# Moving the loads of the units' weights from SyncE's queue to ScalarE's, 0.3 slots later, in a hybrid attention block

## The chip, the cores and the metric

The kernel runs on one core of a Trainium2 chip. The metric is the device time of one execution in microseconds, as the median of several runs. The names of the engines are those of the profile: PE (TensorE), PEld (its weight loads), DVE (VectorE), ACT (ScalarE), POOL (GpSimd) and SP (SyncE, which computes nothing here and only issues DMAs).

## The reference

One layer works on x of 2048 tokens by 1024 channels in float32. What it computes, cut to what matters:

```python
h = rms_norm(x, norm_gain)
proj = h @ w_in                      # q, k, v of two mixers, gate paths, merge gates
qa, ka, va, qb, kb, vb, ga, gb, mg = split(proj)
ya = banded_attention(norm(qa) * scale, norm(ka), va, 128, 1, bias, sink) * silu(ga)
for g, (window, dilation) in enumerate(((128, 1), (512, 4), (2048, 16))):
    outs[g], lses[g] = dilated_group(norm(qb[g]) * scale, norm(kb[g]), vb[g], window, dilation, bias)
yb = sum(softmax(lses) * outs) * silu(gb)
merged = sigmoid(mg_a + b) * (ya @ w_branch_a) + sigmoid(mg_b + b) * (yb @ w_branch_b)
out = x + merged @ w_out
```

## The kernel before

Every product that needs float32 accuracy is made of float16 halves: an operand is split into a high and a low part, and three matmuls (high x high, low x high, high x low) replace one. The normed input lies in SBUF as XH and XL.

**Units and slots.** The main loop has 14 units (`UNITS`): two of mixer A and twelve of mixer B, each with 384 columns of the input projection, that is, the q, k and v of a few heads. A unit has 8 slots; in each slot a `Pair` projects two blocks of 128 tokens (2 x 24 matmuls of 384 columns, L709), and the attention of earlier blocks is worked off in between. Some slots also carry a fill: a product of the gate paths (L333).

**From projection to attention.** ACT takes the projection out of PSUM (`evac_qk` L726, `v_hi` L735) and DVE ends that with `v_lo` (L741). The bank is then free for PE; there are two such banks (`pj`). q and k are normed, split (ACT L777, DVE L781), swapped (POOL L786) and turned by a DMA transpose into the ring `kq` (`turn`, L794, issued by SP). The scores (L879) read `kq`. Then come bias and maximum (DVE L894), exponentials (ACT L902), their two halves (ACT L907, DVE L911) and another DMA transpose into `pt` (L917, SP). The values' product (L928) reads that, and ACT evacuates it (L951, L956, L960). For two of mixer B's three groups the result `z` is stored to DRAM (`z_store`, L967) by a DMA that ACT issues; all other DMAs are issued by SP.

**The units' weights.** While unit u runs, the weights of unit u+1 are made ready. `w_load` (L182 to L188) loads them in four quarters of 384 KB into the one buffer `wraw`; POOL multiplies each quarter with the norm's gain (`w_gain`, L193), ACT sums squares (L235), and ACT and DVE split it (L252, L258). The buffer `wraw` also serves other loads within a unit (gate weights, L347; pieces of other weights, L1137), so a load first waits for its last reader. Index u+1 = 14 loads the first of the merge gates' weights (`w_mrg`, quarters of 256 KB), index 15 the second; index 0 is loaded before the main loop.

**What sets the order.** Nothing is scheduled automatically. Every step is put with `at(time, f)` into a heap, the time in slots, and the program is recorded in the order of these times; each engine works its instructions off in that order. `W_STEP` and `B_GAP` place the weights' steps: quarter i of unit u+1 is loaded at slot 8u + W_STEP[0] + 0.25 i, its gain is due from 8u + 1.558 on, 0.445 slots apart. So a DMA that waits holds up everything that its issuing engine has queued behind it. All DMAs share eight semaphores in turn, so an issue also waits until the DMA eight places earlier in the program has landed.

Of the kernel before, what the change touches and what calls it, by code (L numbers as in the profile page):

```python
# [61 lines left out]
NU = len(UNITS)  # L62
# [13 lines left out]
Y_DMA = (-0.097, 0.45, 0.55, 1.05, 1.13, 1.2, 1.25)  # L76
Y_MAX_DMA = (0.026, 1.4, 1.45)
GATE = (-0.123, -0.064, 0.329)
W_STEP = (0.1, 0.465, 1.9, 0.445, 4.197, 0.146, 0.342)
W_MAX = (3.762, 3.892)  # L80
G_PREP = (5.907, 6.882, 7.102, 7.671, 7.712, 7.812, 7.942)
N_PREP = (6.3, 7.15, 7.753)
# [41 lines left out]
def block_kernel(tc, x, w_units, w_gate, w_mrg, w_brn, w_out, w_bra, gain, qkg, sink, bias_a, bias_b, b_merge, out):  # L124
    nc = tc.nc
# [53 lines left out]
    def raw_tile():  # L179
        return wp.tile([128, NCH, 384], F32, name="wraw", bufs=1)  # L180

    def w_load(u, parts=(0, 1, 2, 3)):  # L182
        if u not in wtiles:
            wtiles[u] = [raw_tile()]
        raw = wtiles[u][0]
        src, n = (w_units[u], 384) if u < NU else (w_mrg[u - NU], 256)
        for i in parts:
            nc.sync.dma_start(out=raw[:, 2 * i:2 * i + 2, :n], in_=src[:, 2 * i:2 * i + 2, :])  # L188

    def gains(raw, c0, n):  # L190

# [243 lines left out]
    def chain(steps):  # L435

        steps = sorted(steps, key=lambda e: e[0])
        done = [0]

        def go(k):  # L440
            if done[0] < k or steps[k][1](*steps[k][2:]) is False:
                at(now[0] + .04, go, k)
            else:
                done[0] = k + 1

        for k, e in enumerate(steps):
            at(e[0], go, k)
# [140 lines left out]
    for i in range(4):  # L588
        at(X_W["ld"][i], w_load, 0, (i,))
# [8 lines left out]
    for pos, c, q, halves in X_MM:  # L598
# [5 lines left out]
        n = 256 * len(halves)  # L604
# [558 lines left out]
    for u in range(NU + 1):  # L1163
        t = 8 * u
        steps = [(t + W_STEP[0] + B_GAP[0] * i, w_load, u + 1, (i,)) for i in range(4)]
        for i in range(4):
            steps += [(t + W_STEP[2] - W_STEP[6] + W_STEP[3] * i, w_gain, u + 1, i),
                      (t + W_STEP[2] + W_STEP[3] * i, w_square, u + 1, i),
                      (t + W_STEP[4] + W_STEP[3] * i, w_hi, u + 1, i),
                      (t + W_STEP[4] + W_STEP[5] + W_STEP[3] * i, w_lo, u + 1, i)]  # L1170
        chain(steps + [(t + d, f, u + 1) for d, f in zip(W_MAX, (w_sum, w_pow))])
# [12 lines left out]
    for k in range(8):  # L1184
        u = 3 + k
# [13 lines left out]
    while t < NPAIR or heap or any(k >= t for k in fill):  # L1199
        u, j = divmod(t, 8)  # L1200
# [211 lines left out]
    def prep(t, u):  # L1412
        sq = [(t + T_W[0], w_load, u), (t + T_W[5], w_sum, u), (t + T_W[6], w_pow, u)]
        for i in range(4):
            sq += [(t + T_W[1] + T_W[2] * i, w_gain, u, i), (t + T_W[3] + T_W[4] * i, w_square, u, i),
                   (t + T_W[7] + T_W[8] * i, w_hi, u, i), (t + T_W[7] + T_W[8] * i + T_W[9], w_lo, u, i)]
        chain(sq)
# [436 lines left out]
```

## Time and profile before

| what | value |
|---|---|
| median of 3 runs (lowest, highest) | 1915.26 us (1915.14, 1917.81) |
| profiled execution, its own time | 1916.12 us |
| its span, first to last instruction | 1914.3 us |
| DMA packets, mean rate over the span | 316.56 MB, 165 GB/s |
| time of SP's queue as a share of 16 DMA engines | 69.2% |
| time of ACT's queue as a share of 16 DMA engines | 2.0% |
| DMAs that ACT issues | 128, all of L967, 66 KB each |
| loads of L188 for the units' weights | 56, 384 KB each; 24 more of 256 KB for `w_mrg` |

How to read it: "q1" in the page is SP's queue and "q10" ACT's. The time from a DMA's issue to its landing is another thing than the duration of the issuing instruction; the profile gives both, the second on the issuing engine's row. A DMA share over 1 is possible in a window, because a packet counts for the time between its start and its end, and packets of one engine overlap.

### The profile page before, as it was taken

The page shows a single profiled execution, that of the slowest core. Times are in us where ns is not written, and L with a number is a line of the kernel's source. Part 1 is how long each engine was busy: PE and PEld are TensorE (multiplying, and loading weights), DVE is VectorE, ACT ScalarE, POOL GpSimd, SP SyncE. Part 2 cuts the span into 40 slices and gives each one's busy share as a digit, 9 for nine tenths or more (in the row PEclk, how much of TensorE's full clock was granted, in tenths as well). Part 3 has the DMA queues.
Part 4 walks back from the last instruction along what each step waited for, and adds up shares of the span by engine and source line. Part 5 has one row for each costly group of instructions (what it writes and reads, how often), then busy time and mean ns, then how long its engine had stood idle before and what let it go on. Part 6 is the DMA issues. An engine that isn't in the chain of part 4 may idle for free.

```text
span 1914.3 us, 39281 instructions
## 1 busy us (share of the span) xinstructions
PE 1899.4 (99%) x13578; PEld 1190.4 (62%) x13578; DVE 1360.3 (71%) x3522; ACT 1120.4 (59%) x2496; POOL 843.7 (44%) x1848
## 2 busy tenths in 40 slices
PE   8999999999999999999999999999999999999999
PEld 6566666677666688566787667876544444444444
DVE  8578886887767877577776877768686667767312
ACT  8468776787656776566766767666544545323100
POOL 4333454344545655446555565555412211223543
DMA  8459986897968697578768788766822346778763
GB/s 285 128 107 181 194 166 152 149 199 151 189 104 197 131 186 139 116 158 175 168 123 155 160 174 150 130 118 132 186 75 99 105 154 220 223 245 261 265 226 138
DMA packets 624585, 316.56 MB, mean 165 GB/s; under 512 B 492928, under 2 KB 562176, under 8 KB 623104
## 3 DMA queue, kind: packets, MB, share of 16 engines
q1 hardware_dynamic: 605952, 305.39, 69.2%
q10 hardware_dynamic: 18432, 8.66, 2.0%
q8 instruction: 106, 1.74, 0.4%
q14 instruction: 95, 0.78, 0.2%
HBM read 129.91 MB, written 65.27 MB: 102 GB/s over the span
## 4 chain that ended last, share of the span: by engine, by line
PE 86%; DVE 5%; DMA 3%; POOL 2%; issue 2%; ACT 2%; SPq 0%; DVEq 0%; POOLq 0%; ACTq 0%
PE pj L709 37%; PE pj L333 15%; PE fps L333 11%; PE fps L1721 6%; PE s L879 5%; PE pv L928 4%; PE fps L1516 3%; DMA kq<-spl 2%; PE pj L1721 2%; PE pj L609 2%; PE pj L1516 1%; DVE p L911 1%; DVE pr L894 1%; DVE qss L753 1%; DVE rw L765 0%
## 5 line engine op out<-in xcount | busy, mean ns | idle before, releaser
L709 PE MATMUL pj<-wh,XL 128*128 128x384 f16 x1792 | 586.1, 327 | 0.0
L709 PE MATMUL pj<-wh,XH 128*128 128x384 f16 x1792 | 584.5, 326 | 1.4 <-DVE vt L741 1.4
L709 PE MATMUL pj<-wl,XH 128*128 128x384 f16 x1792 | 584.7, 326 | 0.0
L709 PEld LDWEIGHTS <-XH 128*128 128x128 f16 x3584 | 410.5, 116 | 151.9 <-issue 1.7
L894 DVE CUSTOM_DVE_ANT_0 pr<-s,b,ubuf 128x256 f32<-128x256 f32 (+3 forms) x512 | 219.1, 465 | 81.1 <-PE s L879 79.3
L709 PEld LDWEIGHTS <-XL 128*128 128x128 f16 x1792 | 207.7, 116 | 70.3 <-issue 1.2
L911 DVE SCALAR_TENSOR_TENSOR p<-pr,p 128x512 f16<-128x512 f32 (+2 forms) x256 | 189.5, 740 | 20.2 <-ACT p L907 20.0
L786 POOL COPY spl<-spl 128x256 f16<-128x256 f16 (+1 forms) x224 | 88.1, 423 | 185.7 <-DVE spl L781 184.3
L726 ACT ACTIVATE rw<-pj 128x256 f32<-128x256 f32 (+1 forms) x224 | 86.8, 388 | 138.3 <-PE pj L709 124.2
L907 ACT ACTIVATE p<-pr 128x512 f16<-128x512 f32 (+2 forms) x256 | 159.2, 622 | 6.2
L333 PEld LDWEIGHTS <-wh 128*128 128x128 f16 x960 | 93.7, 98 | 110.5
L879 PE MATMUL s<-kq 128*128 128x256 f16 (+3 forms) x1168 | 147.8, 254 | 2.9 <-DMA kq<-spl 2.9
L928 PEld LDWEIGHTS <-pt 128*128 128x128 f16 x3024 | 125.4, 97 | 34.8
L286 POOL TENSOR_TENSOR rs_t<-rs_y 128x8 f32<-128x8 f32 (+1 forms) x112 | 40.2, 359 | 238.4 <-DVE rs_y L278 189.6
L771 POOL TENSOR_TENSOR rw<-rw,g 128x256 f32<-128x256 f32 (+1 forms) x112 | 90.8, 811 | 109.9 <-DVE rw L765 76.1
L193 POOL TENSOR_TENSOR wraw<-wraw,gn 128x768 f32<-128x768 f32 (+1 forms) x80 | 112.5, 1411 | 55.5 <-DMA wraw<-in_w_mrg_dram 43.6
L928 PE MATMUL pv<-vt,pt 128*128 128x65 f16 (+1 forms) x3024 | 132.7, 192 | 0.0
L879 PEld LDWEIGHTS <-kq 128*128 128x128 f16 x1184 | 101.5, 98 | 45.5 <-DMA kq<-spl 4.4
L765 DVE TENSOR_TENSOR rw<-rw,qr 128x512 f32<-128x512 f32 (+1 forms) x112 | 103.6, 925 | 30.8 <-POOL qr L295 29.9
L741 DVE SCALAR_TENSOR_TENSOR vt<-pj,vt 128x128 f16<-128x128 f32 (+1 forms) x224 | 62.1, 277 | 88.3 <-ACT vt L735 87.4
L333 PE MATMUL pj<-XH,gh 128*128 128x512 f16 x320 | 121.3, 379 | 0.0
L333 PE MATMUL pj<-XH,gl 128*128 128x512 f16 x320 | 121.2, 379 | 0.0
(281 smaller groups left out, 3799.0 us busy)
## 6 DMA issues: line engine op xcount, KB each, us to landing
wraw<-in_w_units_dram SPq DMA_DIRECT2D x56, 384.0 KB, 4.8
mtd<-mm SPq DMA_DIRECT2D x56, 256.0 KB, 3.7
M<-mtd SPq DMA_DIRECT2D x8, 1792.0 KB, 9.5
mgd<-fg SPq DMA_DIRECT2D x39, 256.0 KB, 2.1
zd<-z ACTq DMA_DIRECT2D x128, 66.0 KB, 2.6
zz<-zd SPq DMA_DIRECT2D x64, 132.0 KB, 2.8
xt<-in_x_dram SPq DMA_DIRECT2D x16, 512.0 KB, 9.4
gtd<-yo SPq DMA_DIRECT2D x32, 256.0 KB, 2.9
```

What stands on the lines that cost most here:

```text
L193: G.tensor_tensor(v, v, gn[:, c0:c0 + 2].unsqueeze(2).to_broadcast([128, 2, n]), OP.mult)
L333: out.append(lambda w=w, xx=xx, ch=ch, i=i: T.matmul(ps[:], lhsT=w[:, ch, c0:c0 + 128], rhs=xx[:, ch, ts], start=(i == 0), stop=(i == n - 1)))
L709: out.append(lambda lhs=lhs, rhs=rhs, ch=ch, k=k: T.matmul(ps[:, :384], lhsT=lhs[:, ch, :], rhs=rhs[:, ch, :], start=(k == 0), stop=(k == ...
L765: V.tensor_tensor(q, q, self.rr[:, :n].unsqueeze(2).to_broadcast([128, n, HD]), OP.mult)
L771: G.tensor_tensor(k, k, GT[un.br][:].unsqueeze(1).unsqueeze(1).to_broadcast([128, 2, un.nk, HD]), OP.mult)
L786: G.tensor_copy(sp[:, i, nh:, :, :], sp[:, i, nq:nh, ::-1, :])
L879: T.matmul(self.sv[j][:, o:o + k1 - k0], lhsT=q[:, h, qo:qo + 128], rhs=kt[:, un.nq + kh + v * un.nk, k0:k1], start=(v == 0), stop=(v == 1))
L894: V.tensor_tensor_reduce(out=self.pv[:, j, self.p0:self.p0 + W], in0=self.sv[j], in1=un.bias[:, self.h0 + j, self.b0:self.b0 + W], scale=I ...
L907: A.activation(self.sp[:, :128 * n], self.pr, AF.Copy, scale=PSC)
L911: V.scalar_tensor_tensor(self.sp[:, 128 * n:], self.pr, PSC, self.sp[:, :128 * n], OP.mult, OP.subtract)
L928: T.matmul(self.po[:, j, :w], lhsT=p[:, n * j + s, :], rhs=un.v[key][:, vh, c0:c0 + w], start=(k == 0 and s == 0), stop=(k == 2 and s == n ...
L1721: mm.append(lambda ch=ch, k=k, w=w, i=i: T.matmul(ps[:, :cols.stop - cols.start], lhsT=m[:, a, ch, k, :], rhs=wt[w][:, b, ch, cols], start ...
```

## The change

`W_STEP[0]`, the place of a unit's first load in the unit in front of it, goes from 0.1 to 0.4 slots, and the loads of indices 1 to 14 are issued by ACT. Index 0 and the merge weights from index 15 on stay on SP; of these only index 15 is placed by `W_STEP`, so it moves by 0.3 slots too.

```diff
-W_STEP = (0.1, 0.465, 1.9, 0.445, 4.197, 0.146, 0.342)
+W_STEP = (0.4, 0.465, 1.9, 0.445, 4.197, 0.146, 0.342)
...
-            nc.sync.dma_start(out=raw[:, 2 * i:2 * i + 2, :n], in_=src[:, 2 * i:2 * i + 2, :])
+            (nc.scalar if 0 < u <= NU else nc.sync).dma_start(out=raw[:, 2 * i:2 * i + 2, :n], in_=src[:, 2 * i:2 * i + 2, :])
```

The instructions of PE, DVE and POOL and their order stay as they are. SP loses 56 DMAs and ACT gains them. On SP, this is what stood at the start of unit 6, when the weights of unit 7 are loaded (around 688 to 701 us in the profile; `b` is the bias table, `kq` the turned q and k, `pt` the turned exponentials):

```order
L674 DMA b_10634<-in_bias_b_dram 128x512
L188 DMA wraw<-in_w_units_dram 128x768
L794 DMA_TRANSPOSE kq<-spl 128x6x128 x2
L188 DMA wraw<-in_w_units_dram 128x768
L917 DMA_TRANSPOSE pt_10711<-p_10646 128x8x128
L188 DMA wraw<-in_w_units_dram 128x768 x2
L917 DMA_TRANSPOSE pt_10792<-p_10739 128x8x128
L794 DMA_TRANSPOSE kq<-spl 128x6x128 x2
```

And this stands there now:

```order
L674 DMA b_10634<-in_bias_b_dram 128x512
L794 DMA_TRANSPOSE kq<-spl 128x6x128 x2
L917 DMA_TRANSPOSE pt_10710<-p_10646 128x8x128
L917 DMA_TRANSPOSE pt_10791<-p_10738 128x8x128
L794 DMA_TRANSPOSE kq<-spl 128x6x128 x2
```

The four loads are gone from between the transposes, and the rest follows in the same order. On ACT this stood at the same place (from about 694.5 us on; `z` and `zd` are the stored result, `rw`, `vt` and `spl` the evacuated projection and its halves):

```order
L907 ACTIVATE p_10739<-pr 128x512
L960 ACTIVATE z<-pv 128x2x65
L967 DMA zd_87<-z 128x132
L777 ACTIVATE spl<-rw 128x2x4x64
L726 ACTIVATE rw<-pj 128x256
L735 ACTIVATE vt<-pj 128x2x64
L748 ACTIVATE spl<-rw 128x512
L902 ACTIVATE pr<-pr,z 128x192 x2
L907 ACTIVATE p_10815<-pr 128x512
L960 ACTIVATE z<-pv 128x2x65
```

And now:

```order
L907 ACTIVATE p_10738<-pr 128x512
L188 DMA wraw<-in_w_units_dram 128x768
L960 ACTIVATE z<-pv 128x2x65
L967 DMA zd_87<-z 128x132
L188 DMA wraw<-in_w_units_dram 128x768
L777 ACTIVATE spl<-rw 128x2x4x64
L726 ACTIVATE rw<-pj 128x256
L735 ACTIVATE vt<-pj 128x2x64
L748 ACTIVATE spl<-rw 128x512
L902 ACTIVATE pr<-pr,z 128x192 x2
L907 ACTIVATE p_10814<-pr 128x512
L188 DMA wraw<-in_w_units_dram 128x768
```

These are quarters 1, 2 and 3 of unit 7; quarter 0 stands a few rows ahead, behind a store of `z`. Quarters 1 and 3 stand behind an L907, quarter 2 behind a store. At the end of the main loop, where the second merge weights are loaded by SP in both kernels (around 1349 to 1357 us), SP's queue had:

```order
L188 DMA wraw<-in_w_mrg_dram 128x2x256
L416 DMA mgd_112<-yo 128x512
L188 DMA wraw<-in_w_mrg_dram 128x2x256
L917 DMA_TRANSPOSE pt_21195<-p_21134 128x8x128
L1031 DMA ytd_97<-yo 128x512
L794 DMA_TRANSPOSE kq<-spl 128x6x128 x2
L941 DMA zz<-zd_89 128x2x132 x2
```

And now:

```order
L188 DMA wraw<-in_w_mrg_dram 128x2x256
L416 DMA mgd_112<-yo 128x512
L188 DMA wraw<-in_w_mrg_dram 128x2x256
L917 DMA_TRANSPOSE pt_21194<-p_21133 128x8x128
L1031 DMA ytd_97<-yo 128x512
L794 DMA_TRANSPOSE kq<-spl 128x6x128 x2
L941 DMA zz<-zd_89 128x2x132 x2
L188 DMA wraw<-in_w_mrg_dram 128x2x256
```

Before, the two loads shown were quarters 2 and 3; now they are quarters 1 and 2, and quarter 3 has come behind the transposes of q and k.

## The prediction

> **What bounds the kernel now.** I read the page first, then the busy time by stage, then who TensorE (PE) waited for, and then the queue that those waits lead to. The page gives the engines' shares:
>
> ```profile
> span 1914.3 us, 39281 instructions
> PE 1899.4 (99%) x13578; PEld 1190.4 (62%) x13578; DVE 1360.3 (71%) x3522; ACT 1120.4 (59%) x2496; POOL 843.7 (44%) x1848
> ```
>
> PE is busy for 1899.4 of 1914.3 us, so 14.9 us are idle. The change leaves PE's instructions and their order alone, so all that it can give is part of that idle time. The stage it acts in runs from 70.4 us (first matmul of unit 0) to about 1424 us (last gate products of the main loop):
>
> ```profile
> 70.40:1424.00 1353.60, 1348.14 (x10898) 927.26 (x10897) 1019.80 (x2937) 897.18 (x2128) 681.86 (x1722) 1.00 0.77 153
> ```
>
> The columns are length, then busy time of PE, weight loads, VectorE (DVE), ScalarE (ACT), GpSimd (POOL), granted clock, DMA share and GB/s. PE idles for 1353.60 - 1348.14 = 5.5 us there; that is the ceiling of any gain. PE's waits in this stage say for what (total us, times, longest):
>
> ```profile
> PE s L879 <- DMA kq<-spl: 2.9, 4, 1.0
> PE pj L709 <- DVE vt L741: 1.4, 1, 1.4
> PE pt L210 <- DVE yo L1023: 0.8, 2, 0.4
> PE pt L210 <- DVE wm L217: 0.4, 1, 0.4
> ```
>
> They sum to 5.5 us. The biggest, 2.9 us, is four scores (L879) that wait for a transposed q/k block, a DMA transpose that SyncE (SP) issues at L794. PE's timeline has them at these four places, with the idle time in brackets:
>
> ```profile
> 704.28 0.61 PE L879 MATMUL s<-kq 128*128 128x256 f16 x4 [0.56 <-DMA kq<-spl]
> ...
> 965.96 0.61 PE L879 MATMUL s<-kq 128*128 128x256 f16 x4 [0.95 <-DMA kq<-spl]
> ...
> 1208.48 0.61 PE L879 MATMUL s<-kq 128*128 128x256 f16 x4 [1.03 <-DMA kq<-spl]
> ...
> 1356.70 0.50 PE L879 MATMUL s<-kq 128*128 128x256 f16 x3 [0.37 <-DMA kq<-spl]
> ```
>
> Ahead of the first, SP's queue shows the weights' loads (L188) close in front of the transposes:
>
> ```profile
> 692.34 0.56 SPq L188 DMA_DIRECT2D wraw<-in_w_units_dram  x1
> ...
> 694.37 1.08 SPq L188 DMA_DIRECT2D wraw<-in_w_units_dram  x2
> 695.99 1.24 SPq L917 DMA_TRANSPOSE pt<-p  x1
> 698.08 2.98 SPq L794 DMA_TRANSPOSE kq<-spl  x2
> ```
>
> The block issued at 698.08 releases PE just before 704.28, so it takes about 6.2 us to land, against a median of 3.2 in the page's list of issues:
>
> ```profile
> kq<-spl SPq DMA_TRANSPOSE x224, 3.2
> ```
>
> The stretches around the first and the third wait, and the stretch that follows the first, differ in DMA share (next to last column; over 1 since packets in flight overlap):
>
> ```profile
> 688.00:707.00 19.00, 18.44 (x160) 16.09 (x157) 15.38 (x46) 13.29 (x36) 11.33 (x30) 1.00 1.15 221
> 707.00:750.00 43.00, 43.00 (x368) 37.76 (x366) 31.73 (x92) 29.09 (x77) 25.30 (x70) 1.00 0.64 114
> 1192.00:1211.00 19.00, 17.97 (x151) 15.62 (x148) 14.87 (x45) 12.14 (x33) 11.44 (x31) 1.00 1.15 213
> ```
>
> 1.15 against 0.64: the DMA engines are saturated when the four loads, the bias load and the transposes meet, and the q/k block stands behind what was issued before it.
>
> **The change part by part.** *Loads off SP.* 56 loads leave SP's queue. What that does for the block at 698.08 depends on which loads are issued ahead of it. SP's pair before it lands like this:
>
> ```profile
> L188 SPq DMA_DIRECT2D wraw<-in_w_units_dram x2: 443/518/593, 694.4 to 695.0; - x2
> ...
> DMA to landing us min/median/max: 5.0/5.2/5.4
> ```
>
> They land at 694.4 + 5.0 = 699.4 and 695.0 + 5.4 = 700.4: one load holds a saturated queue for about 1.0 us. ACT's timeline tells where the new issues fall:
>
> ```profile
> 695.07 0.26 ACT L960 ACTIVATE z<-pv 128x130 f32<-128x130 f32 x1
> 695.36 0.33 ACTq L967 DMA_DIRECT2D zd<-z  x1
> 695.73 0.63 ACT L777 ACTIVATE spl<-rw 128x512 f16<-128x512 f32 x1 [0.40 <-POOL rw L771]
> ...
> 698.04 0.64 ACT L907 ACTIVATE p<-pr 128x512 f16<-128x512 f32 x1
> ```
>
> In the new order load 1 stands just ahead of the L960 of 695.07 and load 2 just behind the store of 695.36, both still ahead of 698.08; load 3 stands behind the L907 of 698.04, so after the transpose. Only one of the four leaves the block's front, so it lands up to 1.0 us sooner. It can be less: loads 0 to 2 come 1 to 3 us later, and if the engines run dry meanwhile the backlog isn't shorter by a whole load. Ends: nothing, or the whole wait. I take the full load, since the share of 1.15 leaves little room to run dry: 0.56 + 0.95 + 1.0 (of 1.03) = 2.5 us. The fourth wait comes amid the loads of the second merge weights (`w_load(15)`), which stay on SP and are only set later; the last of them falls behind that transpose, so of 0.37 I take 0.3 (ends 0 and 0.37). Gain: 2.8 us.
>
> Does a DMA that ACT issues stand in the same line? One that ACT issued in the third stretch, a 66 KB store, and the pair of loads just ahead of it on SP:
>
> ```profile
> L188 SPq DMA_DIRECT2D wraw<-in_w_units_dram x2: 440/509/578, 1196.9 to 1197.5; - x2
> ...
> DMA to landing us min/median/max: 6.1/6.3/6.5
> ```
>
> ```profile
> zd<-z ACTq DMA_DIRECT2D x128, 66.0 KB, 2.6
> ```
>
> ```profile
> L967 ACTq DMA_DIRECT2D zd<-z x1: 326/326/326, 1197.8 to 1197.8; - x1
> ...
> DMA to landing us min/median/max: 7.2/7.2/7.2
> ```
>
> It took 7.2 us where 2.6 is its median, and landed at 1205.0, after the second load (1197.5 + 6.5 = 1204.0). So ACT's queue did not get past SP's backlog: landing went by time of issue. By this, SP's transposes would not wait for a load that ACT issues after them.
>
> The Trainium skill, DMA: Bandwidth & Descriptors, section Queues, rings and completion order, says otherwise: each engine takes turns between the queues that have work, a packet at a time. By that rule a late load shares the engines with a transpose issued just before it, and the sum would lose most of its 2.8 us; it is the first rival.
>
> *Loads onto ACT.* On SP an issue took a median of 0.53 us; on ACT the store's took 0.33:
>
> ```profile
> L188 SPq DMA_DIRECT2D wraw<-in_w_units_dram x56: 328/529/1521, 14.1 to 1197.5; - x56
> ```
>
> Whether this stops ACT depends on what stands ahead. Behind a long ACTIVATE the issue runs under it, behind a short one the next instruction waits:
>
> ```profile
> 322.98 0.83 ACT L235 ACTIVATE wl<-wraw 128x768 f16<-128x768 f32 x1
> 323.11 0.33 ACTq L967 DMA_DIRECT2D zd<-z  x1
> ...
> 323.82 0.74 ACT L777 ACTIVATE spl<-rw 128x640 f16<-128x640 f32 x1
> ```
>
> Here L777 starts as L235 ends, nothing is lost; at 695.36 above, behind an L960 of 0.26, ACT idled 0.40. In the order shown, two of a unit's four loads stand behind a store or a short copy and two behind a 0.6 us ACTIVATE: about 2 x 0.4 = 0.8 us of delay per unit. ACT was idle 19.00 - 13.29 = 5.7 us in the 688 to 707 stretch, so the delay is soon absorbed. What is queued behind an issue on ACT are the PSUM evacuations (L726, L735), which PE needs back. I looked for the tightest such place beside a load, in unit 2:
>
> ```profile
> 293.62 0.22 ACT L735 ACTIVATE vt<-pj 128x64 f16<-128x64 f32 x1
> ```
>
> ```profile
> 295.05 0.22 DVE L741 SCALAR_TENSOR_TENSOR vt<-pj,vt 128x64 f16<-128x64 f32 x1
> ```
>
> ```profile
> 295.62 0.33 PE L709 MATMUL pj<-wh,XL 128*128 128x384 f16 x1
> 295.78 0.33 PE L709 MATMUL pj<-wh,XH 128*128 128x384 f16 x1
> ```
>
> PE reuses the bank at 295.78, 0.5 us after VectorE let go (295.27); VectorE started 1.2 us after ACT was done (293.84). A delay of 0.8 fits in 1.2. I charge 0.2 us for all units. Upper end: at a full 0.53 each, 2.1 us against 1.2 + 0.5 = 1.7 leaves 0.4 at a place like this; four such places make 1.6.
>
> *Waits of the moved issue.* SP waited at L188 for the buffer's last reader, at most this long:
>
> ```profile
> SPq L188 <- DVE gl L386: 4.4, 4, 1.8
> ```
>
> A slot is 48 projection matmuls 0.16 us apart, 7.8 us; 0.3 of it is 2.3 us, more than 1.8, so ACT finds the buffer free. And nothing stands on a load soon: GpSimd scales that unit's quarters from 702.1 to 714.9, and load 3 at about 698.7 feeds the last one; with the 7.2 us of the slowest landing above it is there by 705.9. Cost nothing; without that cover (landing over 16 us) the split of the weights would be late.
>
> ```profile
> L193 POOL TENSOR_TENSOR wraw<-wraw,gn x4: 1459/1467/1467, 702.1 to 714.9; 128x768 f32<-128x768 f32 x4
> ```
>
> **Sum.** -2.8 + 0.2 = -2.6 us. The profiled execution took 1916.12 us, 1.8 more than its span, and lies 0.9 above the median of the runs, 1915.26. On its own terms it becomes 1913.5; from the median, 1912.7.
>
> **The rivals.**
> - *Nothing gained.* The late loads share the engines with the transposes, or the engines run dry for the microsecond saved; the waits stay. For: the share is 1.15 in either order, since the bytes are the same. Against: the store of 7.2 us. Time: 1915.3 + 0.2 = 1915.5.
> - *ACT blocks (slower).* An issue on ACT stretches in a backlog as SP's did, to 1.5 us (1521 ns). Loads 1 and 2, one store apart, then delay ACT by 3.0 us, which at margins of 1.7 leaves 1.3 per unit; if half of 14 units meet such a margin, 9 us: 1924. It decides when two issues together pass 1.7 us, 0.85 each. Against: the store at 1197.8 took 0.326 us in the thick of a backlog.
> - *More than the transposes' waits go.* With SP free of 56 issues and the order shifted, some of the VectorE waits of 1.4 + 0.8 + 0.4 us go too: 1915.3 - 4.2 = 1911.1. Against: none of them names SP, a DMA or ACT.
>
> **How the numbers follow.** Forecast 0.58, nothing gained 0.24, ACT blocks 0.11, more goes 0.07. About 0.2%, 3.8 us, is what a measurement of this kernel can tell from no change. The forecast and the first rival lie within it; only the third passes it downwards (0.08 with a little scatter), only the second upwards (0.11); same 0.81. The range starts at the third rival, 1911.0, and ends at the first with the whole upper cost, 1915.5 + 1.4 = 1916.9, widened to 1917.8, where one run of before lies; ACT blocking is left out.
>
> **What would show it.** Right: the three waits at 704, 966 and 1208 are gone or under 0.2 us; those q/k blocks land in 5 to 6.5 us; L188 appears on ACT's queue at 0.33 to 0.6 us each; PE idles under 3.5 us between 70 and 1424 us. Wrong: the waits stay though the loads moved (the first rival); or PE newly waits for L735 or L741 beside the loads (the second); or a wait of GpSimd for the loaded tile.

## The result, and the profile after

The changed kernel takes 1919.22 us (median of 20 runs, 1915.81 to 1927.35) where the kernel before takes 1915.58 beside it (20 runs, 1913.88 to 1920.87): a ratio of 1.0021, 95% interval 1.0014 to 1.0027. It is slower by 3.6 us, and that lies above the predicted range. The profiled execution took 1919.93 us.

PE stays the bound, and the two queues have changed as intended. From the page of the changed kernel, the span, the engines, and SP's (q1) and ACT's (q10) queue:

```profile
span 1918.1 us, 39272 instructions
...
PE 1900.2 (99%) x13578; PEld 1190.9 (62%) x13578; DVE 1358.8 (71%) x3522; ACT 1119.5 (58%) x2496; POOL 845.7 (44%) x1848
...
q1 hardware_dynamic: 597376, 283.89, 65.4%
q10 hardware_dynamic: 27008, 30.16, 6.2%
```

PE's busy time is the same within 0.8 us (1899.4 before), so the loss is idle time. The stage from unit 0's first matmul to the end of the main loop, which now ends 4 us later:

```profile
70.40:1428.00 1357.60, 1348.20 (x10898) 927.30 (x10897) 1019.88 (x2937) 896.27 (x2128) 683.33 (x1722) 1.00 0.77 152
```

PE idles 1357.60 - 1348.20 = 9.4 us here, against 5.5 before. These 3.9 us are the whole growth of the span (1918.1 - 1914.3 = 3.8). PE's waits in the changed kernel say where they are:

```profile
PE s L879 <- DMA kq<-spl: 6.0, 3, 2.7
PE pj L709 <- DVE vt L741: 2.2, 3, 1.4
PE pt L210 <- DVE yo L1023: 0.8, 2, 0.4
PE pt L210 <- DVE wm L217: 0.4, 1, 0.4
```

The wait for q/k blocks, which was to go, doubled from 2.9 to 6.0 us; the wait for VectorE's `v_lo` grew by 0.8; the other two stayed. Place by place in PE's timeline:

```profile
296.70 0.32 PE L709 MATMUL pj<-wh,XH 128*128 128x384 f16 x1 [0.66 <-DVE vt L741]
...
707.28 0.61 PE L879 MATMUL s<-kq 128*128 128x256 f16 x4 [2.65 <-DMA kq<-spl]
...
970.77 0.61 PE L879 MATMUL s<-kq 128*128 128x256 f16 x4 [2.75 <-DMA kq<-spl]
...
1212.07 0.60 PE L879 MATMUL s<-kq 128*128 128x256 f16 x4
...
1360.55 0.61 PE L879 MATMUL s<-kq 128*128 128x256 f16 x4 [0.65 <-DMA kq<-spl]
```

The waits that were 0.56 and 0.95 are 2.65 and 2.75; the 1.03 near 1208 is gone; the 0.37 at the end is 0.65. For the first of these, the load that ACT issued and the block that SP issued, each with its time to landing:

```profile
L188 ACTq DMA_DIRECT2D wraw<-in_w_units_dram x1: 334/334/334, 699.9 to 699.9; - x1
...
DMA to landing us min/median/max: 7.3/7.3/7.3
```

```profile
L794 SPq DMA_TRANSPOSE kq<-spl x1: 1209/1209/1209, 698.7 to 698.7; - x1
...
DMA to landing us min/median/max: 8.5/8.5/8.5
```

The block was issued 1.2 us ahead of load 3, and both land at 707.2. It took 8.5 us against 6.2 before. What the 16 DMA engines did in the changed kernel while the block was under way, first from 699 to 701 us, then from 704 to 705.5; the columns are packets, MB and share of the engines' time:

```profile
q10 hardware_dynamic: 322, 0.56, 79.5%
q1 hardware_dynamic: 31, 0.01, 1.7%
```

```profile
q10 hardware_dynamic: 47, 0.12, 88.7%
q1 hardware_dynamic: 286, 0.07, 26.9%
```

In the first stretch ACT's queue has the engines nearly to itself. But its 0.56 MB are more than the 384 KB of load 3: loads 1 and 2, which ACT had issued ahead of the block, are still under way:

```profile
L188 ACTq DMA_DIRECT2D wraw<-in_w_units_dram x2: 340/392/445, 694.4 to 695.9; - x2
...
DMA to landing us min/median/max: 6.1/6.3/6.5
```

They land at 700.9 and 702.0, and from 701 to 703 us SP's queue moves 1504 packets. In the second stretch load 3 is under way beside the block: ACT's queue takes 88.7% of the engines' time, and both queues together move 0.19 MB in 1.5 us, against 0.57 MB in the 2 us of the first. What the engines spend that time on, the trace does not tell. That loads on ACT's queue hold up the blocks on SP's, load 3 above all, is the theory to be tested.

### The profile page after: what moved, and what is told of

The parts are those of the page before. It is cut to its first block, busy times and chain, and to the rows that moved or that the text cites. A ratio compares the mean times of both kernels' runs of the same rounds, so it can differ in the third digit from the quotient of the medians.

```text
span 1918.1 us, 39272 instructions
## 1 busy us (share of the span) xinstructions
PE 1900.2 (99%) x13578; PEld 1190.9 (62%) x13578; DVE 1358.8 (71%) x3522; ACT 1119.5 (58%) x2496; POOL 845.7 (44%) x1848
## 4 chain that ended last, share of the span: by engine, by line
PE 85%; DVE 5%; DMA 3%; issue 2%; POOL 2%; ACT 2%; SPq 0%; DVEq 0%; ACTq 0%; POOLq 0%
PE pj L709 37%; PE pj L333 14%; PE fps L333 11%; PE fps L1721 6%; PE s L879 5%; PE pv L928 4%; PE fps L1516 3%; PE pj L1721 2%; DMA kq<-spl 2%; PE pj L609 2%; PE pj L1516 1%; DVE pr L894 1%; DVE p L911 1%; DVE qss L753 1%; DVE spl L781 0%
## 5 line engine op out<-in xcount | busy, mean ns | idle before, releaser
L907 ACT ACTIVATE p<-pr 128x512 f16<-128x512 f32 (+2 forms) x256 | 159.2, 622 | 6.9 <-DMA pt<-p 0.7
L193 POOL TENSOR_TENSOR wraw<-wraw,gn 128x768 f32<-128x768 f32 (+1 forms) x80 | 112.7, 1414 | 55.8 <-DMA wraw<-in_w_mrg_dram 44.1
L741 DVE SCALAR_TENSOR_TENSOR vt<-pj,vt 128x128 f16<-128x128 f32 (+1 forms) x224 | 62.1, 277 | 86.2 <-ACT vt L735 85.3
```

The source lines that it names most:

```text
L193: G.tensor_tensor(v, v, gn[:, c0:c0 + 2].unsqueeze(2).to_broadcast([128, 2, n]), OP.mult)
L907: A.activation(self.sp[:, :128 * n], self.pr, AF.Copy, scale=PSC)
```

## The experiments

Three theories: **turns** (the engines serve two queues by turns, and a load on ACT's queue takes them away from the transposes on SP's, also from those issued earlier), **shift** (the place 0.3 slots later does it, on any queue), and **ACT's issues** (issuing delays the evacuations). Each kernel was timed beside the kernel before, whose median was 1915.2 to 1915.3. A profile shows one execution; for the engine alone, the last quarter on ACT and the loads behind the block on ACT it is the slowest of the runs.

**The shift alone.** The loads at 0.4 slots, all issued by SP.

```diff
-            (nc.scalar if 0 < u <= NU else nc.sync).dma_start(
+            nc.sync.dma_start(
```

> The loads go 0.3 slots later but all stay on SP, one queue in order of issue. Three theories stand for the 3.6 us that the change lost. Turns: the DMA engines take from ACT's queue and SP's in turn, so that loads on ACT's queue hold up a q/k block that SP issued before them; then the shift alone costs nothing: load 3 now stands behind the block on the same queue, the waits for q/k blocks near 704, 966 and 1208 us are 0 to 1.0 us each, the time 1913 to 1916 us. Shift: it is the later place that puts the loads among the transposes, on whichever queue; then the waits near 704 and 966 are about 2.8 us as in the changed kernel and the time is 1918 to 1920. ACT's issues: they delay the evacuations; none are on ACT here, so 1915 to 1916 with the waits of before.

It took 1913.59 us (11 runs, 1912.68 to 1914.14), ratio 0.9993 (0.9984 to 1.0002). PE's waits, and the q/k pair near 698 us:

```profile
PE pj L709 <- DVE vt L741: 1.4, 1, 1.4
PE s L879 <- DMA kq<-spl: 1.2, 1, 1.2
```

```profile
L794 SPq DMA_TRANSPOSE kq<-spl x2: 1212/1732/2252, 697.8 to 699.1; - x2
...
DMA to landing us min/median/max: 5.3/5.3/5.4
```

The three waits near 704, 966 and 1208 are gone; the blocks land in 5.3 us instead of 6.1, and load 3, now behind them on the same queue, in 4.1. The shift does not lose time. It even does what the whole change was predicted to do; one wait near 1353 us grew, to 1.2.

**The engine alone.** The loads on ACT at the old 0.1 slots.

```diff
-W_STEP = (0.4, 0.465, ...
+W_STEP = (0.1, 0.465, ...
```

> The loads go to ACT but stay at 0.1 slots. Turns: the loads on ACT's queue take engines from SP's transposes here too, but all four are issued before the q/k block (695 against 698 us), so much of their bytes is through by then; waits near 704, 966 and 1208 of 0.5 to 2 us, time 1916 to 1918. Shift: the place is the old one, so the waits are those of before (0.6 to 1.0) and the time is 1915 to 1916. ACT's issues: as in the changed kernel or worse, since the first load now waits on ACT for the buffer's reader, up to 1.8 us: new waits of PE for VectorE's L741 of 1 us or more in all, time 1917 or more with the q/k waits as before.

It took 1926.37 us, ratio 1.0051 (1.0037 to 1.0065), far above what turns gave for it. Its waits:

```profile
PE s L879 <- DMA kq<-spl: 9.8, 6, 3.2
PE pj L709 <- DVE vt L741: 4.8, 5, 2.6
PE pj L709 <- ACT yo L408: 1.7, 1, 1.7
```

The waits for q/k blocks, 9.8 us, are the largest, so shift is out, for the place is the old one, and so is ACT's theory as the whole cause, which had these waits as before. The 4.8 us for L741 are what ACT's theory had asked for, but ACT itself waits 30.9 us for q/k blocks here, 3.3 in the kernel before, so they need not come from its issuing. Turns were under-priced, at 1916 to 1918; how the other 6.5 us divide was not taken apart.

**Three units back.** Loads of units 7, 10 and 13 on SP at 0.1, the rest on ACT at 0.4.

```diff
+            (nc.scalar if 0 < u <= NU and u not in (7, 10, 13) else nc.sync).dma_start(
...
+        steps = [(t + (0.1 if u + 1 in (7, 10, 13) else W_STEP[0]) + B_GAP[0] * i, w_load, u + 1, (i,)) for i in range(4)]
```

> The changed kernel, but the loads of units 7, 10 and 13 (those beside the q/k waits near 704, 966 and 1208) go back to SP at 0.1 slots; the other eleven stay on ACT at 0.4. Turns, and shift likewise: the waits near 704 and 966 go from 2.8 and 2.9 back to 0.6 to 1.1, the one near 1208 comes back with about 1.0, and PE's waits for L741 near 89 and 296 us (0.33, 0.83) stay if they come from other units' loads; time 1916 to 1917. ACT's issues: 44 of 56 issues stay on ACT, so most of the loss stays, 1918 or more.

1916.32 us, ratio 1.0009 (1.0000 to 1.0017). The q/k waits fell to 2.7 us, near the 2.9 of before, though they sit elsewhere (1.6 of them near 704, none near 1208). So with 44 loads on ACT the time stays about 1 us over before; the rest of the loss goes with the 12 of these three units.

**The last quarter on SP.** Three loads of a unit on ACT, the fourth, issued behind the q/k block, on SP.

```diff
+            (nc.scalar if 0 < u <= NU and i < 3 else nc.sync).dma_start(
```

> The changed kernel, but of each unit's four loads the last is issued by SP, where it stands behind the q/k block; three stay on ACT. Turns: nothing that is issued after the block can pass it on SP's own queue, so the waits near 704 and 966 fall from 2.8 and 2.9 to 0 to 1.2 us; time 1915 to 1917. Shift: as many bytes at the same time, waits of 2 us and more stay, 1918 to 1920. ACT's issues: three quarters of the loss stay, about 1918, as PE's waits for L741.

1915.53 us, ratio 1.0002 (0.9993 to 1.0010). One load in four, moved back to the block's own queue, takes away the loss:

```profile
PE pj L709 <- DVE vt L741: 3.4, 2, 1.7
PE s L879 <- DMA kq<-spl: 1.0, 2, 0.7
```

The waits near 704 and 966 are 0, and the block near 704 lands in 4.9 us. What stays over the shift alone is mainly a wait for L741 near 297 us. Its origin is in ACT's timeline: a row of the kernel before, one of the changed kernel, one of this.

```profile
291.16 0.52 ACT L806 ACTIVATE kq<-kq 128x384 f16<-128x384 f16 x1 [1.83 <-DMA kq<-spl]
```

```profile
292.54 0.52 ACT L806 ACTIVATE kq<-kq 128x384 f16<-128x384 f16 x1 [3.10 <-DMA kq<-spl]
```

```profile
293.28 0.52 ACT L806 ACTIVATE kq<-kq 128x384 f16<-128x384 f16 x1 [4.15 <-DMA kq<-spl]
```

ACT copies part of each q/k block within the ring (L806). In both kernels with loads on ACT's queue that copy waits longer for the transpose, and L907, L735 and then VectorE's L741 come late behind it. So this wait too begins with a slow transpose, not with ACT's issuing.

**The last quarter on ACT.** The reverse: only the fourth load on ACT.

```diff
+            (nc.scalar if 0 < u <= NU and i == 3 else nc.sync).dma_start(
```

> The reverse of the last quarter on SP: at 0.4 slots three loads of a unit stay on SP and only the fourth, the one that is issued just after the q/k block, goes to ACT. Turns: this one load is enough; the waits near 704 and 966, which were 0 with all four on SP at these places, are 1 to 2.5 us; time 1914.5 to 1917. If all of ACT's loads together are needed to fill the engines, the waits stay under 0.3 and the time is that of the shift alone, 1913.6.

1921.10 us (9 runs), ratio 1.0027 (1.0017 to 1.0037): 14 loads on ACT cost 7.5 us over the shift alone. Waits, the place near 966 in PE's timeline, the queues from 962 to 964 us, and PE in the 3.2 us that follow the wait:

```profile
PE s L879 <- DMA kq<-spl: 7.1, 3, 3.2
```

```profile
967.48 1.03 PE L879 MATMUL s<-kq 128*128 128x256 f16 x4 [3.24 <-DMA kq<-spl]
```

```profile
q10 hardware_dynamic: 105, 0.30, 82.4%
q1 hardware_dynamic: 58, 0.01, 10.5%
```

```profile
967.30:970.50 3.20, 3.02 (x11) 1.74 (x12) 1.50 (x5) 0.35 (x2) 0.38 (x2) 0.50 0.88 188
```

Turns hold, and for more than expected: two waits are 3.2 us, the time is over the 1917 allowed, and after the wait near 966 the granted clock is 0.50, so the matmuls take about twice as long for a while. In four stretches of 3.2 us behind the two long waits the clock was 0.50, 0.55, 0.62 and 0.84; by these, an estimate, 4.8 us are lost. With 5.9 us more of q/k waits than in the shift alone that makes 10.7 of the 10.9 us between the two spans (1922.9 and 1912.0).

Near 1208 load 3 was issued 0.1 us after the block, which took 9.5 us. Near 966 it was issued 0.4 us ahead of the block, but 1.7 us behind a transpose of exponentials, which took 10.1 us where it takes 5.3 in the shift alone: so here too the load holds up what was issued before it. Near 704 the block takes 6.0 us and PE does not wait; in the changed kernel it waits there and not near 1208. What decides which block is hit stays open.

**Short packets.** The changed kernel, each load of units 1 to 13 as two DMAs of 192 columns, so packets of 768 bytes, not 3072.

```diff
+            for c in ((slice(0, 192), slice(192, 384)) if 0 < u < NU else (slice(0, n),)):
+                (nc.scalar if 0 < u <= NU else nc.sync).dma_start(out=raw[:, 2 * i:2 * i + 2, c], in_=src[:, 2 * i:2 * i + 2, c])
```

> The changed kernel, but each load of a quarter is split into two DMAs of half the columns, so that its packets have 768 bytes in place of 3072; all still on ACT's queue at 0.4 slots, eight issues a unit. The run before this showed that it is the loads on the second queue that hold up SP's q/k blocks; open is why they win. Size: the engines take a packet from each queue in turn, so a queue of long packets moves many more bytes per turn than the transposes with their 256; at 768 bytes the load's advantage falls from 12 to 1 to 3 to 1 and the waits near 704 and 966 go from 2.8 and 2.9 to about 1 to 2; time 1916 to 1918. Queue: ACT's queue is served first or as often whatever the size, the transposes wait for the whole load; waits of 2.5 us and more, time 1919 to 1922 (the 56 more issues add up to 0.5).

1916.27 us, ratio 1.0005 (0.9996 to 1.0014). Waits (lines are 1 higher here):

```profile
PE pj L710 <- DVE vt L742: 2.6, 2, 2.1
...
PE s L880 <- DMA kq<-spl: 0.4, 2, 0.2
```

This points to the packets' size, not to the queue's rank: with packets a quarter as long, and as many bytes on the same queue, the block near 704 lands in 5.4 us in place of 8.5 and the waits for q/k blocks are 0.2 each, less than the 1 to 2 expected. It is not proof, since each DMA is also half as big and there are twice as many of them; long packets in half-size DMAs were not tried. Twice as many issues on ACT did not undo the gain. The kernel still takes 2.7 us more than the shift alone; part of that is a longer wait for L742, 2.1 us near 1099, and a slow clock behind it (below).

**Small issues on ACT.** Loads on SP at 0.4 slots, and 56 ACT issues of 512 bytes beside them.

```diff
+            nc.sync.dma_start(out=raw[:, 2 * i:2 * i + 2, :n], in_=src[:, 2 * i:2 * i + 2, :])
+            if 0 < u <= NU:
+                nc.scalar.dma_start(out=tiny[4 * u + i:4 * u + i + 1, :], in_=idf[0:1, :])
```

> The loads stay on SP at 0.4 slots, as in the shift alone (1913.6 us), and beside each of the 56 ACT issues a DMA of one row of 512 bytes to a scratch in DRAM that nobody reads: ACT's cost of issuing without the bytes. Turns: the issues cost ACT some tenths of a us each, which its slack takes up; 1913.5 to 1914.5 us, no new wait of PE for L741 above 0.3 us, q/k waits near 704 and 966 still 0. ACT's issues: if these themselves delayed the evacuations, the waits for L741 near 89 and 296 us (0.3 and 0.8 in the changed kernel) come back and the time is 1915 or more.

1913.51 us, ratio 0.9992 (0.9983 to 1.0001), against 1913.59 without the issues. PE's waits (lines are 3 higher here):

```profile
PE pj L712 <- DVE vt L744: 1.9, 2, 1.4
...
PE s L882 <- DMA kq<-spl: 0.2, 1, 0.2
```

One new wait of 0.5 us for L744 stands near 90 us, more than the 0.3 allowed; the changed kernel has one of 0.17 there. The one near 296 does not come. Issuing costs nothing that the time shows.

**Behind the block.** All four loads at 1.15 to 1.21 slots, behind the second q/k block of a unit's start: once on ACT, once on SP.

```diff
-        steps = [(t + W_STEP[0] + B_GAP[0] * i, w_load, u + 1, (i,)) for i in range(4)]
+        steps = [(t + (1.15 + 0.02 * i if u < NU else W_STEP[0] + B_GAP[0] * i), w_load, u + 1, (i,)) for i in range(4)]
```

> All four loads of a unit are issued by ACT right behind the second q/k block of a unit's start (1.15 to 1.21 slots), so that all 1.5 MB come after it in the program. The loads are later than in any kernel so far, which may make GpSimd wait for them by some us; the next kernel has the same places on SP, and only the difference of the two counts. Turns: the load's bytes pass the block; the q/k waits of PE near 704 and 966 are 3 to 6 us each (one load more for each 1.0 to 1.4 us), with others like them at other units; time 1922 or more, 6 or more over the SP version. Order of issue: what is issued behind the block cannot hold it up, waits under 0.3, the same time as the SP version within 1 us.

> The same places behind the q/k block, on SP. Turns and order of issue alike: on one queue the block is ahead of the loads, q/k waits near 704 and 966 are 0 to 0.3; the exponentials' transposes and the next q/k blocks now stand behind 1.5 MB, so new waits of 1 to 3 us may come a few us later, and GpSimd may wait for the loads; time 1912.5 to 1918.

On ACT 1933.28 us (4 runs), ratio 1.0094 (1.0081 to 1.0108); on SP 1919.44, ratio 1.0022 (1.0013 to 1.0032): the queue alone makes 13.8 us. PE's waits on ACT, then on SP:

```profile
PE pj L709 <- DVE vt L741: 7.4, 6, 2.6
PE s L879 <- DMA kq<-spl: 5.6, 4, 3.6
PE pv L928 <- DMA pt<-p: 4.1, 2, 2.8
```

```profile
PE pj L709 <- DVE vt L741: 3.8, 3, 2.6
PE pv L928 <- DMA pt<-p: 3.7, 2, 2.7
...
PE s L879 <- DMA kq<-spl: 0.5, 1, 0.5
```

The total came out as turns had it, the places only in part: with loads on ACT the q/k waits are not those of the blocks near 704 and 966 but of later ones (3.6 us near 981). On SP the loads cost as well, 4.1 us over before and more than the 1918 allowed. The next transposes stand behind them there: the one on which the wait near 431 us hangs, issued 0.5 us after the last load, took 9.1 us. GpSimd waits 35.4 us for the loads on SP and 4.9 on ACT; PE has no wait for them.

**Later on SP, without the merge weights.** The shift alone, but index 15 at 0.1 slots.

```diff
+        steps = [(t + (W_STEP[0] if u < NU else 0.1) + B_GAP[0] * i, w_load, u + 1, (i,)) for i in range(4)]
```

> The shift without the engine, for the units 1 to 14 alone: loads on SP at 0.4 slots, but index 15, the second merge weights, stays at 0.1. By the profile of the shift alone its one q/k wait, 1.3 us near 1352 us, goes back to the 0.5 of before, and the waits near 704, 966 and 1208 stay gone: 1912.5 to 1913.2 us, some 2 to 2.8 below before. If the wait at 1352 was not load 15's doing, 1913.6 as the shift alone.

1913.79 us, ratio 0.9993 (0.9984 to 1.0002): ten runs took 1912.62 to 1914.81, the eleventh 4283.15, and the ratio leaves that one out. The expectation failed: the wait near 1353 fell, but one of 0.7 us near 1205 came, where the shift alone has none with the same instructions. Single waits of under 1 us differ so much between executions that one profile does not price them.

## Why the prediction was wrong

The point that failed is in "Loads off SP": "landing went by time of issue. By this, SP's transposes would not wait for a load that ACT issues after them." The block issued at 698.7 took 8.5 us, and load 3, which ACT issued at 699.9, took 7.3. With only that load back on SP the block took 4.9; with all four on SP, block and load took 5.4 and 4.1. So a load that ACT issued later did delay SP's transposes, and PE's waits near 704 and 966 grew from 0.56 and 0.95 to 2.65 and 2.75 us. The evidence for that step was one store of 66 KB that did not get past SP's backlog; a load of 384 KB in packets of 3072 bytes did hold that backlog up, and the short packets suggest that packet length matters. The store was the wrong stand-in; why it in particular was slow was not tested. Loads 1 and 2, which the prediction counted as ahead of the block on either queue, took 6.5 and 6.1 us on ACT's, 4.5 and 5.1 in the shift alone; how much of the block's 8.5 us is theirs was not taken apart.

The other steps:
- **The bound held.** All that changed is PE's idle time in the main loop, +3.9 us.
- **A load fewer in front of the block** was right, at 1.7 us where 2.5 was put for these three waits: on one queue they all went (the shift alone), but the time fell by less, also since the wait near 1353 grew. With it, the change divides into -1.7 for the place and about +5.6 for the queue (1919.2 - 1913.6).
- **The fourth wait**, 0.3 predicted as gain, grew by 0.3; it varied from 0.2 to 1.2 in kernels with the same instructions there.
- **ACT's issues**, 0.2 us, were small as predicted: an issue has a median of 340 ns in the changed kernel, and 56 issues alone cost nothing measurable. The second rival, slower because ACT blocks, had the sign and not the cause.
- **Nothing stood on a load** was right: PE never waited for the tile, nor GpSimd at L193 for a load of the units' weights.
- **The first rival** named the rule and took it to leave the waits as they were, 1915.5. They doubled. It had the late loads give back what the earlier ones gained and no more; the two blocks took 8.4 to 8.5 us, about 2 us more than before the change (6.2 and 6.6).

The rule of that rival, the Trainium skill, DMA: Bandwidth & Descriptors, section Queues, rings and completion order (an engine takes turns between the queues that have work, a packet at a time), points the right way, and the short packets speak for it. Whether the turns are equal the runs do not show. From 704 to 705.5 us 47 packets of ACT's queue took 88.7% of the engines' time and 286 of SP's 26.9%, and whether a packet of the profile is one turn is not known.

## What to carry to other kernels

A bulk load that is issued from a second engine does not queue up behind urgent small transfers on the first: here it held them up even when issued later. Where the engines are as busy as here, keep bulk loads on the queue of the transposes; with the last of a unit's four loads behind the urgent one that gained 1.7 us, and with all four behind it lost 4.1, because other transposes then stood behind them. Shorter packets took back most of the loss, not all. Before one transfer's latency is taken as a sign for another, compare their sizes and packet lengths.

## What the runs showed of the hardware

PE's clock. After the wait of 3.24 us above the granted clock was 0.50. It also fell after shorter ones, and not after all. The windows behind a wait of 2.7 us and behind one of 2.6 in the kernel with the loads behind the block on SP, and behind one of 2.1 in the kernel with short packets:

```profile
431.00:434.20 3.20, 3.13 (x26) 2.07 (x27) 1.55 (x2) 3.06 (x6) 0.93 (x1) 0.55 1.22 314
...
1105.00:1108.20 3.20, 3.01 (x20) 2.20 (x20) 3.03 (x14) 0.90 (x3) 2.24 (x8) 1.00 0.39 73
```

```profile
1099.70:1103.30 3.60, 3.56 (x13) 1.92 (x13) 2.86 (x11) 0.74 (x3) 2.48 (x10) 0.53 0.76 182
```

The Trainium skill, TensorE: Matmul & The Clock Gate, Part 1, has the clock halved after an idle window of about 3.4 us that runs freely. The halving agrees; here one wait of 2.1 us sufficed, and one of 2.75 did not. In the changed kernel's profile the clock stayed at 1.00 after 2.65 and 2.75 us, but 7 of its 20 runs had a mean clock of 0.998 or 0.999 and took 1919.8 to 1927.4 us, the other 13, at 1.000, 1915.8 to 1920.5. So part of its loss, in some runs, is probably a slow stretch behind a wait; none of these seven was profiled.

The kernels with all loads on SP at 0.4 slots took 1913.5 to 1913.8 us as medians, and each of their runs but the one of 4283.15 lies below the median of before; no single ratio among them excludes 1.
